# Layer 0's S5 parameter preparation spread among the mixers' turns, LRU first, three column tiles with the first norm

## The chip, the cores and the metric

The kernel runs on one core of one Trainium2 chip. The metric is the device time of one execution in microseconds (us); the kernel before takes 1784.58 us, the median of three runs (1783.12 to 1785.43). Engines: PE is TensorE, DVE VectorE, ACT ScalarE, POOL GpSimd, SP the engine that issues the transfers (DMA).

## What is computed

Two layers of a hybrid backbone over 640 tokens (128 of a context pass, 512 of a denoising step) of 1024 channels, in fp32. Cut to what matters:

```python
mod = silu(cond) @ mod_w + mod_b                    # six vectors of 1024: shift, scale, gate, twice
h = rmsnorm(x, norm1_w) * (1.0 + sc1) + sh1
proj = h @ w_in                                     # 20 column tiles of 128
ya, st_a = ssd_mixer(pa, ...)                       # Mamba-2 SSD, chunks of 128 tokens
yb, st_b = retention_mixer(pb, ...)
yc, st_c = s5_mixer(pc, ...)                        # complex diagonal scan
yd, st_d = lru_mixer(pd, ...)                       # RG-LRU, diagonal scan
y = concatenate([ya, yb, yc, yd]) @ w_out
x = x + g1 * y
h = rmsnorm(x, norm2_w) * (1.0 + sc2) + sh2
x = x + g2 * conv_ffn(h, w_up, conv_w, conv_b, w_down)
```

S5 needs parameters that depend on no token: `abar = exp(lam * step)`, its powers, `bbar = coef * b`, and `c` times powers. The kernel computes them on the chip.

## The kernel before, in words

Activations lie with channels on the partitions, in 8 tiles of 128 channels (k = 0 to 7), each as a high and a low part (`hhi`, `hlo`); weights are split the same way by `wsplit`: SP loads a `raw` page of 128x512, ACT casts it to `hi`, DVE or POOL (by turns) subtracts to `lo`. `mm3` multiplies three of the four pairs. A column tile (`col_tile`) is 128 output columns for all 640 tokens in two halves of 320, each half in a PSUM bank: 8 k x 3 products x 2 halves = 48 matmuls of 128x320, and two raw pages. There are 3 banks for column tiles ("mm"), 1 "a", 2 "b", 1 "c", 1 "mod".

Layer 0 starts with nothing in place. `mod_first(q)` computes the shift and scale for two of the eight k at a time (q = 0 to 3), with matmuls into `mod` and then DVE steps (`modtt`, `modtl`, eight copies of 32x4 into `mod0`). The norm then makes, per k, `nt` on DVE, `hhi` on ACT and `hlo` on DVE or POOL. `first_tiles` (L232) builds the first two column tiles (S5's) quarter by quarter as the norm's channels arrive.

After that each mixer is a generator; `ORDER` lists their turns (L45 of the kernel before), one `yield` to the next per turn, and after each turn `filler` steps the computation of layer 0's other four modulation vectors (`mod_units`, matmuls `mod<-mraw,s`). In layer 0 the S5 mixer goes first, and the whole of `s5_prep(0)` (L577) is emitted behind its first step. `s5_prep` makes powers and tables (`pw`, `tab`, `tbr`), then for each of four q the products `pmr` and `pt` of 128x512 on DVE with `pmi` and `pt` on POOL, transposes on PE (`c`), and copies on ACT (`wbs`, `kt`, `kk`). `s5_mixer` (L773) copies the two column tiles out of PSUM on ACT (`s5cp`, `s5cs`), transposes them (`b`, `s5u`), and runs scans per q (`s5a`, `s5r`) with the prepared matrices (`wb`, `wc`, `tb`). SSD's chunks run as `sE`, `S` and `scb` steps on DVE with PE.

The program's order on each engine is not the emitted one: a scheduler orders instructions by a model of their times, within the dependencies, and pages and banks of one tag are handed out in the emitted order (`fresh`, `last`). An engine runs its queue in that order. All operations pass through one recording helper (L92 before, L90 after), so every row shows that line and the tiles' names tell which step it is.

Of the kernel before, what the change touches and what calls it, by code (L numbers as in the profile page):

```python
# [9 lines left out]
F32 = mybir.dt.float32  # L10
# [7 lines left out]
P = 128  # L18
# [7 lines left out]
HO = (1, 0)  # L26
# [12 lines left out]
TSR = 1  # L39
LB = 1  # L40
FPS = 2
ST = 'AAC'
MR = 'C'

ORDER = ("s5 gb lru lru gb ssd ssd z lru ssd z ret ret ssd ret ssd ret ret ret ret",  # L45
         "s5 ssd gb lru ssd lru gb z lru ssd z ret ssd ret ret ssd ret ret ret ret")
RAWS = 5
SPLITS = 5
# [27 lines left out]
def hybrid_kernel(ctx: ExitStack, tc: tile.TileContext, I, O, dbg=None):  # L76
# [155 lines left out]
    def first_tiles(units, act, steps=None):  # L232


        ws = [wsplit(u, 1024, le=G) for u in units]
        out = [[None, None] for _ in ws]
        for ks in steps or ():
            for h in HO:
                for i, (w, o) in enumerate(zip(ws, out)):
                    if o[h] is None:  # L240
                        o[h] = bank("a" if i and h == HO[1] else "mm")
                    col_tile(w, act, halves=(h,), ks=ks, out=o[h])
        if steps:
            return out
        for h in HO:
            for w, o in zip(ws, out):
                o[h], = col_tile(w, act, halves=(h,))
        return out


    s4 = cst.tile([P, 8, 32], F32, name="s4")
# [7 lines left out]
    def mod_first(q):  # L259

        ps = bank("mod")
        for k in range(8):
            if k % 2 == 0:
                raws = [page(MR, name="mraw")[:, :512] for _ in range(2)]
                for c in range(2):
                    SP.dma_start(raws[c], I["mod0"][q, c, k // 2])
            for c in range(2):
                j = 2 * (k % 2) + c
                T.matmul(ps[32 * j:32 * j + 32, 0:256], s4[:, k, :], raws[c][:, 256 * (k % 2):256 * (k % 2) + 256],
                         start=k < 2, stop=k > 5, tile_position=(0, 32 * j))  # L270
        tt = smp.tile([P, 16, 32], F32, tag="modtt", name="modtt")[:, 0:8]
        V.transpose(tt, ps[:, 0:256].rearrange("p (b r) -> p b r", r=32))
        tl = smp.tile([64, 16, 2], F32, tag="modtl", name="modtl")[:, 0:8]
        V.tensor_copy(tl, tt[64:128, :, 0:2])
        V.tensor_tensor(tl, tl, tt[0:64, :, 0:2], op=ALU.add)
        ks = slice(2 * q, 2 * q + 2)
        for c in range(2):
            src = tl[32 * c:32 * c + 32].rearrange("p (q b) d -> p q b d", b=4)
            for b in range(4):
                V.tensor_copy(mod0[32 * b:32 * b + 32, c, ks, :], src[:, :, b, :])  # L280
        V.tensor_tensor(mod0[:, :, ks], mod0[:, :, ks],
                        pr(0, "mod_b", 0, 16).rearrange("p (c k) -> p c k", c=2)[:, :, ks].unsqueeze(3).to_broadcast(
                            [P, 2, 2, 2]), op=ALU.add)
        mod_scale(0, 0, ks)

    def mod_units(l, c, pages):


        ps = bank("mod")
        after = mybir.DependencyInfo(mybir.DependencyClass.Sync, mybir.DependencyReason.DATA)  # L290
        for k in range(8):
            raws = [page(pages, name="mraw")[:, :512] for _ in range(2)]
            dmas = [SP.dma_start(raws[i], I["mod_w"][l, c, k, :, 512 * i:512 * i + 512]) for i in range(2)]
            for j in range(4):
                mm = T.matmul(ps[32 * j:32 * j + 32, 0:256], s4[:, k, :], raws[j // 2][:, 256 * (j % 2):256 * (j % 2) + 256],
                              start=k == 0, stop=k == 7, tile_position=(0, 32 * j))
                if j < 2:
                    tc.add_manual_dep(mm.ins, dmas[1].ins.name, after, reason="four at a time")
            if k < 7:
                yield  # L300
        tt = smp.tile([P, 16, 32], F32, tag="modtt", name="modtt")[:, :8]
        V.transpose(tt, ps[:, 0:256].rearrange("p (b r) -> p b r", r=32))
        dst = modT[l][c]
        for j in range(4):
            src = tt[32 * j:32 * j + 32, :, 0:2].rearrange("p (q b) c -> p q b c", b=4)
            for b in range(4):
                V.tensor_copy(dst[32 * b:32 * b + 32, 2 * j:2 * j + 2, :], src[:, :, b, :])
        V.tensor_tensor(dst, dst, pr(l, "mod_b", c * 8, 8).unsqueeze(2).to_broadcast([P, 8, 2]), op=ALU.add)
        yield

# [266 lines left out]
    def s5_prep(l):  # L577

        wb, wc, tb, zz = s5d[l]
        p1, p2, p3 = "CCC" if l else ST  # L580

        def keep(name, shape):
            return smp.tile([P] + shape, F32, tag=f"k_{name}", name=name)
# [186 lines left out]
            SP.dma_start(zz[:, :, j, :], kk[16 * j:16 * j + 16, :, 16:32])  # L770


    def s5_mixer(l, hh, y, steps):  # L773
        u = []
        yield
        tiles = first_tiles([I["w_in"][l, 4 + i] for i in range(2)], hh, steps)
        for i in range(2):

            ucp, ucs = paged("B", [2, 4, 32], "s5cp"), paged("B", [2, 2, 4, 32], "s5cs")
            G.memset(ucp, 0.0)  # L780
            with tc.high_priority(EVP):
                for h, t, c0, o, n in ((0, ucp, 0, 0, 128), (0, ucs[:, 0], 0, 128, 192), (1, ucs[:, 0], 24, 0, 64),
                                       (1, ucs[:, 1], 0, 64, 256)):
                    A.copy(t[:, :, :, c0:c0 + n // 8],
                           tiles[i][h][:, o:o + n].rearrange("p (c b j) -> p j b c", b=4, j=2)[:, ::-1, ::-1, :])
            uq = paged("B", [8, TB], "s5u")
            ps = bank("b")
            for j in range(2):
# [134 lines left out]
    def lru_mixer(l, hh, y):  # L923
# [14 lines left out]
        hs = []  # L938
        for i in range(2):
            yield  # L940
            pss = col_tile(wsplit(I["w_in"][l, i], 1024), hh)
            raw = page("A", name="lraw")
            evac_padded(pss, raw)
            xr = page("A", name="lxc")
# [53 lines left out]
    def gates(l, hh, units, out, func):  # L998

        for i in range(2):  # L1000
            yield
            pss = col_tile(wsplit(I["w_in"][l, units[i]], 1024), hh)
            for h in range(2):
                o, w = HALF[h]
                if func is None:
# [334 lines left out]
    def layer(l, norm):  # L1340
# [3 lines left out]
        for ks in steps or (range(8),):  # L1344
            if l == 0 and ks[0]:
                mod_first(ks[0] // 2)
            for h in HO:
                norm.apply(l, 0, h, hh, ks)
        ys = {n: [page(tag, name="y" + n) for _ in range(2)] for n, tag in (("lru", "Ya"), ("ssd", "Yb"), ("s5", "Yc"))}
        ys["ret"] = []  # L1350
        gens = {"s5": s5_mixer(l, hh, ys["s5"], steps), "lru": lru_mixer(l, hh, ys["lru"]), "ssd": ssd_mixer(l, hh, ys["ssd"]),
                "ret": ret_mixer(l, hh, ys["ret"]), "gb": gates(l, hh, (2, 3), ys["lru"], AF.Gelu_apprx_tanh),
                "z": gates(l, hh, (9, 11), ys["ssd"], None if TSZ else AF.Silu)}
        for n in gens:
            if n != "ret":
                step(n + str(l), gens[n])
            if l == 0 and n == "s5":
                step("s50", gens[n])
                sec[0] = "prep"
                for _ in s5_prep(0):  # L1360
                    pass
        order = ORDER[l].split()
        for i, n in enumerate(order):
            if n == "ret" and "ret" not in order[:i]:
# [2 lines left out]
                ys["ret"] += [page("Yd", name="yret") for _ in range(2)]  # L1367
                step(n + str(l), gens[n])
            step(n + str(l), gens[n])
            if i == 0 and l == 0:  # L1370
                load_x(0)
            if l == 0 and i >= 1:
                filler(FPS)
# [348 lines left out]
```

## Time and profile before

| | |
|---|---|
| median of three runs | 1784.58 us (1783.12 to 1785.43) |
| the profiled execution | 1781.99 us, span of its instructions 1780.0 us |
| PE busy | 1662.9 us (93%), 11288 matmuls |
| DVE, ACT, POOL busy | 1117.3 (63%), 683.6 (38%), 610.6 us (34%) |
| mean granted clock of PE | 0.974 of full speed |
| transfers | 206.5 MB, mean 116 GB/s |

A busy share over the whole span mixes stages: the FFN, on PE alone, takes most of it. The rows further down are times from the span's start. In a timeline row a bracket tells how long the engine was idle before the instruction and which one ended that; `x8` are eight instructions merged into one row. [...]

### The profile page before, as it was taken

How to read it: one execution, taken by the hardware profiler on the slowest of the kernel's cores; microseconds unless marked ns; L12 is line 12 of the kernel's file. 1: busy time of each engine (PE TensorE's matmuls, PEld its weight loads, DVE VectorE, ACT ScalarE, POOL GpSimd, SP SyncE). 2: the span in 40 equal slices, each digit the busy share in tenths (PEclk: the TensorE clock that was granted, in tenths of full speed). 3: DMA queues.
4: the chain of work that ended last, by engine and by line, in shares of the span. 5: the costliest groups of instructions: out<-in, count | busy, mean ns of one | idle time of the engine just before them, and what ended most of it. 6: DMA issues, size and time to landing. Idle time of an engine off the chain costs nothing. (4 is left out here: it accounts for less than half of the span.)

```text
span 1780.0 us, 30854 instructions
## 1 busy us (share of the span) xinstructions
PE 1662.9 (93%) x11288; PEld 1525.9 (86%) x11288; DVE 1117.3 (63%) x2605; ACT 683.6 (38%) x1448; POOL 610.6 (34%) x838
## 2 busy tenths in 40 slices
PE   4598998999999999999999999999989999999997
PEld 1386787888998988989998889887889999999996
DVE  9977976977543875584447688687764333333345
ACT  4534424444431352232234464454453233233234
POOL 4665343423311263261123344433331121121222
PEclk8798999999999999999999999999999999999998
DMA  8355565321424354444443334422122222222321
GB/s 308 112 182 157 165 202 171 96 81 46 139 81 154 123 173 148 155 152 134 151 138 107 95 121 132 130 85 70 35 63 63 75 84 64 91 72 62 93 73 59
DMA packets 143434, 206.50 MB, mean 116 GB/s; under 512 B 22852, under 2 KB 64692, under 8 KB 143284
## 3 DMA queue, kind: packets, MB, share of 16 engines
q1 hardware_dynamic: 143284, 204.54, 36.7%
q8 instruction: 89, 1.46, 0.3%
q14 instruction: 61, 0.50, 0.1%
HBM read 184.42 MB, written 20.07 MB: 115 GB/s over the span
## 5 line engine op out<-in xcount | busy, mean ns | idle before, releaser
L92 PE MATMUL mm<-hhi,hi 128*128 128x320 f32 x1976 | 625.1, 317 | 34.6 <-ACT hhi L92 28.2
L92 PE MATMUL mm<-hlo,hi 128*128 128x320 f32 x1976 | 627.0, 318 | 7.5 <-DVE hlo L92 4.8
L92 PE MATMUL mm<-hhi,lo 128*128 128x320 f32 x1976 | 619.3, 314 | 1.1 <-DVE lo L92 1.1
L92 ACT CAST hi<-raw 128x512 fp32r<-128x512 f32 (+1 forms) x384 | 227.5, 593 | 606.6 <-PE mm L92 404.1
L92 POOL TENSOR_TENSOR lo<-raw,hi 128x512 fp32r<-128x512 f32 (+1 forms) x200 | 260.4, 1303 | 580.8 <-ACT hi L92 563.2
L92 PEld LDWEIGHTS mm<-hhi,hi 128*128 128x128 f32 x1976 | 376.1, 191 | 58.4 <-ACT hhi L92 33.5
L92 PEld LDWEIGHTS mm<-hlo,hi 128*128 128x128 f32 x1976 | 376.6, 191 | 19.0 <-DVE hlo L92 6.9
L92 PEld LDWEIGHTS mm<-hhi,lo 128*128 128x128 f32 x1976 | 376.7, 191 | 5.4 <-issue 2.4
L92 DVE TENSOR_TENSOR lo<-raw,hi 128x512 fp32r<-128x512 f32 (+1 forms) x184 | 133.7, 727 | 180.9 <-ACT hi L92 165.3
L92 DVE SCALAR_TENSOR_TENSOR x<-mm,mod,x 128x320 f32<-128x320 f32 (+2 forms) x288 | 116.9, 434 | 203.0 <-PE mm L92 201.9
L92 PE MATMUL mm<-fah,hi 128*128 128x320 f32 x640 | 196.8, 313 | 1.0 <-DVE fa L92 0.7
L92 PE MATMUL mm<-fal,hi 128*128 128x320 f32 x640 | 197.4, 309 | 0.0
L92 PE MATMUL mm<-fah,lo 128*128 128x320 f32 x640 | 196.7, 309 | 0.0
L92 PEld LDWEIGHTS mm<-fah,hi 128*128 128x128 f32 x640 | 119.3, 188 | 11.7 <-issue 7.6
L92 PEld LDWEIGHTS mm<-fah,lo 128*128 128x128 f32 x640 | 120.2, 188 | 0.4 <-issue 0.4
L92 PEld LDWEIGHTS mm<-fal,hi 128*128 128x128 f32 x640 | 120.3, 188 | 0.2 <-issue 0.2
L92 DVE TENSOR_TENSOR fa<-fc,mm 128x128 f32<-128x128 f32 x132 | 45.1, 373 | 106.7 <-PE mm L92 103.4
L92 PE MATMUL mod<-mraw,s 128*32 128x256 f32 x768 | 74.4, 414 | 17.5 <-DMA mraw<-in_mod 13.6
L92 DVE SCALAR_TENSOR_TENSOR fc<-fraw,par,fc 128x643 f32<-128x643 f32 x88 | 84.6, 963 | 2.8
L92 POOL MEMSET fraw<- 128x2 f32 x132 | 8.8, 102 | 173.1 <-DVE fc L92 167.3
L92 PE MATMUL mm<-ylo,hi 128*128 128x320 f32 x192 | 61.5, 321 | 1.8 <-DVE ylo L92 1.8
L92 PE MATMUL mm<-yhi,hi 128*128 128x320 f32 x192 | 61.9, 326 | 0.6 <-DVE x L92 0.4
(363 smaller groups left out, 2619.4 us busy)
## 6 DMA issues: line engine op xcount, KB each, us to landing
raw<-in_up SPq DMA_DIRECT2D x176, 256.0 KB
mraw<-in_mod_w SPq DMA_DIRECT2D x160, 256.0 KB
raw<-in_w_in SPq DMA_DIRECT2D x80, 256.0 KB
raw<-in_dn SPq DMA_DIRECT2D x96, 192.0 KB
mraw<-in_mod SPq DMA_DIRECT2D x32, 256.0 KB
raw<-in_w_o SPq DMA_DIRECT2D x32, 256.0 KB
tb<-tb SPq DMA_DIRECT2D x16, 326.0 KB
x<-in_x SPq DMA_DIRECT2D x16, 320.0 KB
```

Source lines behind the costliest of these rows:

```text
L92: r = f(*a, **k)
```

## The change

`ORDER[0]` puts LRU first and S5 behind LRU's third turn; `p` is one step of `s5_prep(0)`, of which there are ten turns. The preparation's large pages come from "B" (12 pages, where S5's `s5cp`, `s5cs` and `s5u` also lie) instead of "A" and "C". The first norm is followed by three column tiles instead of two, LRU's two and the first of its gate, kept in `early` until their turn fetches them (`unit_tile`); the third tile's weight parts lie in pages "A", and the `lo` parts go to DVE and POOL by turns. Layer 1 still starts with S5's two. `mod_first` copies the PSUM rows out on ACT, transposes them on PE into bank "c" and adds them on DVE in two steps. Layer 0's remaining modulation vectors are placed by ACT copies instead of DVE copies. `load_x(0)` follows the second S5 turn instead of the first turn.

```diff
--- before.py
+++ after.py
@@ -39,10 +39,8 @@
 TSR = 1
 LB = 1
 FPS = 2
-ST = 'AAC'
-MR = 'C'
-
-ORDER = ("s5 gb lru lru gb ssd ssd z lru ssd z ret ret ssd ret ssd ret ret ret ret",
+
+ORDER = ("lru p gb p lru p gb p ssd p ssd p z p lru p p p s5 s5 ssd z ret ret ssd ret ssd ret ret ret ret",
          "s5 ssd gb lru ssd lru gb z lru ssd z ret ssd ret ret ssd ret ret ret ret")
 RAWS = 5
 SPLITS = 5
@@ -232,13 +230,14 @@
     def first_tiles(units, act, steps=None):
 
 
-        ws = [wsplit(u, 1024, le=G) for u in units]
+        ws = [wsplit(u, 1024, le=None if steps else G, tag="A" if i > 1 else None) for i, u in enumerate(units)]
         out = [[None, None] for _ in ws]
+        banks = (("mm", "mm"), ("b", "b"), ("a", "mm"))
         for ks in steps or ():
             for h in HO:
                 for i, (w, o) in enumerate(zip(ws, out)):
                     if o[h] is None:
-                        o[h] = bank("a" if i and h == HO[1] else "mm")
+                        o[h] = bank(banks[i][h])
                     col_tile(w, act, halves=(h,), ks=ks, out=o[h])
         if steps:
             return out
@@ -247,6 +246,12 @@
                 o[h], = col_tile(w, act, halves=(h,))
         return out
 
+    early = {}
+
+    def unit_tile(l, u, hh):
+
+        return early.pop((l, u), None) or col_tile(wsplit(I["w_in"][l, u], 1024), hh)
+
 
     s4 = cst.tile([P, 8, 32], F32, name="s4")
     G.memset(s4, 0.0)
@@ -261,26 +266,25 @@
         ps = bank("mod")
         for k in range(8):
             if k % 2 == 0:
-                raws = [page(MR, name="mraw")[:, :512] for _ in range(2)]
+                raws = [page("AC"[q % 2], name="mraw")[:, :512] for _ in range(2)]
                 for c in range(2):
                     SP.dma_start(raws[c], I["mod0"][q, c, k // 2])
             for c in range(2):
                 j = 2 * (k % 2) + c
                 T.matmul(ps[32 * j:32 * j + 32, 0:256], s4[:, k, :], raws[c][:, 256 * (k % 2):256 * (k % 2) + 256],
                          start=k < 2, stop=k > 5, tile_position=(0, 32 * j))
-        tt = smp.tile([P, 16, 32], F32, tag="modtt", name="modtt")[:, 0:8]
-        V.transpose(tt, ps[:, 0:256].rearrange("p (b r) -> p b r", r=32))
-        tl = smp.tile([64, 16, 2], F32, tag="modtl", name="modtl")[:, 0:8]
-        V.tensor_copy(tl, tt[64:128, :, 0:2])
-        V.tensor_tensor(tl, tl, tt[0:64, :, 0:2], op=ALU.add)
+
+        rows = smp.tile([P, 512], F32, tag="modtt", name="modtt")[:, 0:256]
+        A.copy(rows, ps[:, 0:256])
+        ps = bank("c")
+        for i in range(2):
+            T.transpose(ps[:, 128 * i:128 * i + 128], rows[:, 128 * i:128 * i + 128], idn)
         ks = slice(2 * q, 2 * q + 2)
-        for c in range(2):
-            src = tl[32 * c:32 * c + 32].rearrange("p (q b) d -> p q b d", b=4)
-            for b in range(4):
-                V.tensor_copy(mod0[32 * b:32 * b + 32, c, ks, :], src[:, :, b, :])
-        V.tensor_tensor(mod0[:, :, ks], mod0[:, :, ks],
+        src = ps[:, 0:256].rearrange("p (k j r) -> p j k r", k=2, j=4)[:, :, :, 0:2]
+        V.tensor_tensor(mod0[:, :, ks], src[:, 0:2],
                         pr(0, "mod_b", 0, 16).rearrange("p (c k) -> p c k", c=2)[:, :, ks].unsqueeze(3).to_broadcast(
                             [P, 2, 2, 2]), op=ALU.add)
+        V.tensor_tensor(mod0[:, :, ks], mod0[:, :, ks], src[:, 2:4], op=ALU.add)
         mod_scale(0, 0, ks)
 
     def mod_units(l, c, pages):
@@ -304,7 +308,8 @@
         for j in range(4):
             src = tt[32 * j:32 * j + 32, :, 0:2].rearrange("p (q b) c -> p q b c", b=4)
             for b in range(4):
-                V.tensor_copy(dst[32 * b:32 * b + 32, 2 * j:2 * j + 2, :], src[:, :, b, :])
+                cp = A.copy if pages == "Yd" else V.tensor_copy
+                cp(dst[32 * b:32 * b + 32, 2 * j:2 * j + 2, :], src[:, :, b, :])
         V.tensor_tensor(dst, dst, pr(l, "mod_b", c * 8, 8).unsqueeze(2).to_broadcast([P, 8, 2]), op=ALU.add)
         yield
 
@@ -577,7 +582,7 @@
     def s5_prep(l):
 
         wb, wc, tb, zz = s5d[l]
-        p1, p2, p3 = "CCC" if l else ST
+        p1 = p2 = p3 = "C" if l else "B"
 
         def keep(name, shape):
             return smp.tile([P] + shape, F32, tag=f"k_{name}", name=name)
@@ -770,11 +775,11 @@
             SP.dma_start(zz[:, :, j, :], kk[16 * j:16 * j + 16, :, 16:32])
 
 
-    def s5_mixer(l, hh, y, steps):
+    def s5_mixer(l, hh, y):
         u = []
         yield
-        tiles = first_tiles([I["w_in"][l, 4 + i] for i in range(2)], hh, steps)
         for i in range(2):
+            tl = unit_tile(l, 4 + i, hh)
 
             ucp, ucs = paged("B", [2, 4, 32], "s5cp"), paged("B", [2, 2, 4, 32], "s5cs")
             G.memset(ucp, 0.0)
@@ -782,7 +787,7 @@
                 for h, t, c0, o, n in ((0, ucp, 0, 0, 128), (0, ucs[:, 0], 0, 128, 192), (1, ucs[:, 0], 24, 0, 64),
                                        (1, ucs[:, 1], 0, 64, 256)):
                     A.copy(t[:, :, :, c0:c0 + n // 8],
-                           tiles[i][h][:, o:o + n].rearrange("p (c b j) -> p j b c", b=4, j=2)[:, ::-1, ::-1, :])
+                           tl[h][:, o:o + n].rearrange("p (c b j) -> p j b c", b=4, j=2)[:, ::-1, ::-1, :])
             uq = paged("B", [8, TB], "s5u")
             ps = bank("b")
             for j in range(2):
@@ -938,7 +943,7 @@
         hs = []
         for i in range(2):
             yield
-            pss = col_tile(wsplit(I["w_in"][l, i], 1024), hh)
+            pss = unit_tile(l, i, hh)
             raw = page("A", name="lraw")
             evac_padded(pss, raw)
             xr = page("A", name="lxc")
@@ -999,7 +1004,7 @@
 
         for i in range(2):
             yield
-            pss = col_tile(wsplit(I["w_in"][l, units[i]], 1024), hh)
+            pss = unit_tile(l, units[i], hh)
             for h in range(2):
                 o, w = HALF[h]
                 if func is None:
@@ -1346,19 +1351,19 @@
                 mod_first(ks[0] // 2)
             for h in HO:
                 norm.apply(l, 0, h, hh, ks)
+        us = (0, 1, 2) if l == 0 else (4, 5)
+        for u, t in zip(us, first_tiles([I["w_in"][l, u] for u in us], hh, steps)):
+            early[l, u] = t
         ys = {n: [page(tag, name="y" + n) for _ in range(2)] for n, tag in (("lru", "Ya"), ("ssd", "Yb"), ("s5", "Yc"))}
         ys["ret"] = []
-        gens = {"s5": s5_mixer(l, hh, ys["s5"], steps), "lru": lru_mixer(l, hh, ys["lru"]), "ssd": ssd_mixer(l, hh, ys["ssd"]),
+        gens = {"s5": s5_mixer(l, hh, ys["s5"]), "lru": lru_mixer(l, hh, ys["lru"]), "ssd": ssd_mixer(l, hh, ys["ssd"]),
                 "ret": ret_mixer(l, hh, ys["ret"]), "gb": gates(l, hh, (2, 3), ys["lru"], AF.Gelu_apprx_tanh),
                 "z": gates(l, hh, (9, 11), ys["ssd"], None if TSZ else AF.Silu)}
         for n in gens:
             if n != "ret":
                 step(n + str(l), gens[n])
-            if l == 0 and n == "s5":
-                step("s50", gens[n])
-                sec[0] = "prep"
-                for _ in s5_prep(0):
-                    pass
+        if l == 0:
+            gens["p"] = s5_prep(0)
         order = ORDER[l].split()
         for i, n in enumerate(order):
             if n == "ret" and "ret" not in order[:i]:
@@ -1367,7 +1372,7 @@
                 ys["ret"] += [page("Yd", name="yret") for _ in range(2)]
                 step(n + str(l), gens[n])
             step(n + str(l), gens[n])
-            if i == 0 and l == 0:
+            if l == 0 and n == "s5" and "s5" in order[:i]:
                 load_x(0)
             if l == 0 and i >= 1:
                 filler(FPS)
```

How this moves instructions, at three places.

DVE in the first norm, the last quarter (q = 3) of `mod_first`, before (`modtt`, `modtl` are its temporaries, `mod0_87` its result, `am` the scale, `nt` the normed activations, `tab` the preparation's tables):

```order
L92 TENSOR_TENSOR modtl_465<-modtl_465,modtt_463 64x16
L92 TENSOR_TENSOR tabt_946<-tab1_945,e5_859 128x256
L92 COPY s5ph_0_112<-tab1_945 64x8
L92 COPY mod0_87<-modtl_465 32x4 x8
L92 TENSOR_TENSOR tab0_944<-tab0_944,tabt_946 128x8x32
L92 TENSOR_TENSOR mod0_87<-mod0_87,par0_75 128x2x4
L92 SCALAR_TENSOR_TENSOR am0_0_98<-mod0_87,par0_75 128x4
L92 TENSOR_SCALAR am0_0_98<-am0_0_98 128x4
L92 SCALAR_TENSOR_TENSOR nt_479<-x_131,am0_0_98,nrs_136 128x320
L92 SCALAR_TENSOR_TENSOR nt_483<-x_133,am0_0_98,nrs_136 128x320
```

and now:

```order
L90 TENSOR_TENSOR wlo_502<-raw_499,whi_501 128x512
L90 TENSOR_TENSOR mod0_87<-c_444,par0_75 128x2x4
L90 TENSOR_TENSOR tabt_1319<-tab1_1318,e1_1115 128x8x2
L90 TENSOR_TENSOR mod0_87<-mod0_87,c_444 128x2x4
L90 TENSOR_TENSOR tab0_1317<-tab0_1317,tabt_1319 128x8x2
L90 SCALAR_TENSOR_TENSOR am0_0_98<-mod0_87,par0_75 128x4
L90 TENSOR_TENSOR lo_1240<-raw_1237,hi_1239 128x512
L90 TENSOR_TENSOR tab0_1317<-tab0_1317,e2_1120 128x8x4
L90 TENSOR_SCALAR am0_0_98<-am0_0_98 128x4
L90 TENSOR_TENSOR tabt_1319<-tab1_1318,e2_1120 128x8x4
L90 SCALAR_TENSOR_TENSOR nt_451<-x_131,am0_0_98,nrs_136 128x320
L90 SCALAR_TENSOR_TENSOR nt_455<-x_133,am0_0_98,nrs_136 128x320
```

The transpose, the copy, the add and the eight small copies are gone from DVE; two adds that read the transposed PSUM bank `c` stand in their place, with weight splits (`wlo`, `lo`) and table steps between.

PE ahead of S5's second column tile, now (`pmr_2003` and `pmi_2004` are the products of the preparation's last q, `mm_2174` is the second half of S5's second column tile; its first half, `mm_2173`, stands 77 rows earlier, behind both halves of the first tile):

```order
L90 MATMUL mod_1605<-mraw_1614,s4_84 32x256 x2
L90 MATMUL mod_1605<-mraw_1615,s4_84 32x256 x2
L90 MATMUL c_2031<-pmr_2003,cm0_1596 32x128 x4
L90 MATMUL c_2031<-pmi_2004,cm1_1597 32x128 x4
L90 MATMUL c_2042<-ct_72,kt_2040 128x128
L90 MATMUL mod_1605<-mraw_1698,s4_84 32x256 x2
L90 MATMUL mod_1605<-mraw_1699,s4_84 32x256 x2
L90 MATMUL mm_2174<-hhi_237,hi_2163 128x320
L90 MATMUL mm_2174<-hlo_238,hi_2163 128x320
L90 MATMUL mm_2174<-hhi_237,lo_2164 128x320
```

Before, S5's tiles were the first column tiles of the program, ahead of all the preparation's transposes; now the transposes of all four q stand between the first three halves and the fourth.

ACT where S5's tiles are copied out of their banks, before (`mm_533` is the second half of S5's first column tile, `tbr` and `cm0` are preparation):

```order
L92 COPY tbr_1005<-tab1_945 64x4x64
L92 ACTIVATE hhi_258<-nt_495,mod0_87 128x192
L92 COPY s5cs_634<-mm_533 128x8x8
L92 COPY s5cs_634<-mm_533 128x256
L92 ACTIVATE nt_495<-nt_495,mod0_87 128x128
L92 COPY tbr_1005<-tab1_945 64x4x64
L92 COPY cm0_1035<-cq_1022 64x16x16 x2
L92 COPY cm1_1036<-ncq_1033 64x16x16 x2
```

and now (`mm_2092` and `mm_2093` are the first tile's halves; `kk` is the preparation's last result per q):

```order
L90 COPY wbs_2018<-c_2013 128x512
L90 COPY wbs_2027<-c_2022 128x512
L90 COPY kt_2040<-c_2031 128x128
L90 COPY kk_1604<-c_2042 128x128
L90 COPY s5cs_2143<-mm_2093 128x8x8
L90 COPY s5cs_2143<-mm_2093 128x256
L90 COPY s5cp_2142<-mm_2092 128x8x16
L90 COPY s5cs_2143<-mm_2092 128x8x24
L90 CAST hi_2780<-raw_2778 128x512
```

The copies that give S5's banks free stood ahead of the first `kk`; they now stand behind the last of the four.

## Rows read from the trace of the kernel before

**Rows 1.** Stretches: start:end, length, busy PE, PEld, DVE, ACT, POOL, clock, DMA share, GB/s

```profile
0.00:50.00 50.00, 22.83 (x128) 10.78 (x128) 45.77 (x260) 21.83 (x49) 22.20 (x41) 0.86 0.85 300
...
50.00:100.00 50.00, 32.89 (x161) 25.70 (x162) 38.47 (x93) 27.80 (x75) 29.86 (x45) 0.76 0.29 96
...
431.10:1780.00 1348.90, 1301.51 (x8885) 1230.28 (x8883) 765.74 (x1675) 494.87 (x1029) 409.03 (x567) 0.99 0.34 104
```

**Rows 2.** Stretches of layer 0's mixers, columns as above

```profile
100.00:200.00 100.00, 90.10 (x629) 70.73 (x628) 85.41 (x152) 41.11 (x77) 61.40 (x79) 0.95 0.62 186
...
184.50:431.10 246.60, 230.10 (x1586) 200.02 (x1585) 196.44 (x472) 103.02 (x232) 94.15 (x119) 0.99 0.41 128
```

**Rows 3.** Waits of PE, 0 to 300 us: total, times, longest

```profile
PE mm L92 <- ACT hhi L92: 24.9, 6, 10.2
...
PE c L92 <- DVE sE L92: 3.8, 1, 3.8
```

**Rows 4.** Timeline of PE, first column tiles: start, us, instruction

```profile
68.25 0.31 PE L92 MATMUL mm<-hhi,hi 128*128 128x320 f32 x1
68.40 0.31 PE L92 MATMUL a<-hhi,hi 128*128 128x320 f32 x1
78.90 0.90 PE L92 MATMUL mm<-hhi,hi 128*128 128x320 f32 x2 [10.19 <-ACT hhi L92]
...
93.45 0.47 PE L92 MATMUL mm<-hhi,hi 128*128 128x320 f32 x1
93.72 0.47 PE L92 MATMUL mm<-hlo,hi 128*128 128x320 f32 x1
...
113.98 0.31 PE L92 MATMUL mm<-hhi,lo 128*128 128x320 f32 x1
```

**Rows 5.** Stretch of the first norm's activations

```profile
33.50:84.80 51.30, 31.52 (x150) 20.08 (x150) 48.93 (x142) 25.06 (x65) 37.00 (x59) 0.71 0.37 123
```

**Rows 6.** Timeline of DVE, first norm

```profile
27.82 2.68 DVE L92 COPY mod<-modtl 32x4 f32<-32x4 f32 x8
...
33.51 2.02 DVE L92 SCALAR_TENSOR_TENSOR nt<-x,am,nrs 128x320 f32<-128x320 f32 x2
...
73.12 2.98 DVE L92 COPY mod<-modtl 32x4 f32<-32x4 f32 x8
...
84.82 2.55 DVE L92 SCALAR_TENSOR_TENSOR nt<-x,am,nrs 128x128 f32<-128x128 f32 x2
```

**Rows 7.** Groups of DVE, 24 to 88 us: busy, mean ns, idle before

```profile
L92 DVE COPY mod<-modtl 32x4 f32<-32x4 f32 x32 | 8.2, 255 | 0.4
...
L92 DVE COPY modtl<-modtt 64x16 f32<-64x16 f32 x4 | 1.6, 396 | 0.1
...
L92 DVE TENSOR_TENSOR lo<-raw,hi 128x512 fp32r<-128x512 f32 x2 | 1.3, 674 | 0.0
...
L92 DVE STREAM_TRANSPOSE modtt<-mod 128x256 f32<-128x256 f32 x3 | 1.3, 440 | 0.0
...
L92 DVE TENSOR_TENSOR modtl<-modtl,modtt 64x16 f32<-64x16 f32 x4 | 1.1, 283 | 0.0
```

**Rows 8.** Groups of DVE, 85 to 200 us; ACT, 24 to 200 us

```profile
L92 DVE TENSOR_TENSOR pt<-ncq,apcw 128x512 f32<-128x512 f32 x4 | 5.5, 1382 | 0.0
...
L92 DVE TENSOR_TENSOR_SCAN lg<-lg,lT 128x644 f32<-128x644 f32 x2 | 3.0, 1496 | 0.0
...
L92 ACT COPY tbr<-tab 64x68 f32<-64x68 f32 x16 | 4.0, 248 | 1.7 <-DVE tab L92 0.7 <-POOL tab L92 0.6
```

**Rows 9.** Timeline of DVE, the preparation's products

```profile
87.30 0.68 DVE L92 TENSOR_TENSOR pt<-bb,apcw 128x512 f32<-128x512 f32 x1
...
105.35 1.54 DVE L92 TENSOR_TENSOR pmr<-bb,apcw 128x512 f32<-128x512 f32 x1
```

**Rows 10.** Groups of DVE, 200 to 330 us

```profile
L92 DVE TENSOR_TENSOR_SCAN s5r<-tb,s5a 64x328 f32<-64x328 f32 x8 | 6.7, 836 | 1.1 <-POOL s5a L92 0.9
...
L92 DVE SCALAR_TENSOR_TENSOR sE<-scb,cum,sE 128x128 f32<-128x128 f32 x12 | 4.9, 443 | 0.0
```

## The prediction

> **What bounds the kernel now.** I read the page's totals through a table of stretches first: where is TensorE (PE) not busy? From 431.1 us on, PE is busy 1301.5 of 1348.9 us [rows 1], so there is nothing to gain there except by starting it earlier; and since the order of instructions is the same in both programs from the second half of layer 0's output projection on, a lead gained before it is carried to the end one for one. The first 100 us hold two rows of 50 us with 22.8 and 32.9 us of PE work [rows 1]: 44 us idle. From 100 to 431 us the idle share is small: 9.9 us in 100 to 200 and 16.5 us in 184.5 to 431.1 [rows 2]. So the whole case lies before 431 us, most of it before 115.
>
> The waits say what PE lacks there: 24.9 us for `hhi`, the normed activations' high part, in 6 waits, the longest 10.2 [rows 3]. The timeline shows that one: PE stops behind 68.40 and goes on at 78.90 [rows 4]. ACT makes `hhi` from `nt`, which VectorE (DVE) makes, and DVE is busy 48.9 of the 51.3 us from the first `nt` to the last [rows 5]. **DVE sets the pace of the first norm**, and one piece stands out: at 73.12 eight copies of 32x4 take 2.98 us, and nt can't start before them [rows 6].
>
> **The first norm's stage.** For each of four quarters `mod_first` now runs a DVE transpose, a copy, an add and eight small copies: 1.3 + 0.4 (the fourth transpose, at the mean of the three), 1.6, 1.1 and 8.2 us, 12.3 in all [rows 7]. The change gives this to an ACT copy and two PE transposes; DVE keeps the bias add and gets a second one of the same size, which I price at the 0.28 us of the old add [rows 7], 1.1 us together. The saving is 11.2 us, 2.8 per quarter. The first quarter's copies stand at 27.82, before the first `nt` at 33.51 [rows 6]; I take 4 us off (2.8 and the steps that queue behind them), so the first `nt` at 29.5. The other three quarters save 8.4. The split of the third tile adds DVE work: five `lo` of 0.67 us instead of two [rows 7], +2.0. The preparation's first product `pmr`, 1.4 us at the price of its kind [rows 8], and four steps of half its width, taken as the same again, move behind the norm: -2.8. So 9.2 of 48.9 us go, and at the same pace (51.3 us for 48.9) the last `nt` comes at 29.5 + 41.6 = **71 us, against 84.82** [rows 6].
>
> PE must follow. The six raw pages of three tiles instead of four stand ahead of the first tile matmul's ACT cast, so it starts a few us later; that costs nothing as long as the last `nt` decides, and PE has 35 us for the 144 matmuls, which take 21 us at a spacing of 0.15 us (68.25 to 68.40) and 39 at the 0.27 of 93.45 to 93.72 [rows 4]. Three tiles are then finished at about 76. The fourth is one more set of 48 matmuls, 7 us at the one spacing and 13 at the other: 85. Before, the fourth tile ends at 114 [rows 4]. **Lead: 29 us** (22 to 31, by the two spacings).
>
> **The preparation's block.** This is what the lead runs into. `ORDER` puts three turns of `p` ahead of the two of `s5`, but the scheduler starts S5's two column tiles long before: their halves hold all three `mm` banks, and the next tile (`mm` 2174) waits until ACT copies one out. ACT does so behind the last of `kk`, the preparation's product, and in pages "B" that the preparation holds too (the order's pieces on PE and ACT). Before, these tiles had the banks first and were copied out ahead of the first `kk`. So PE now waits for DVE's chain from the last `nt` to the last `pmr`. I count that chain in the change's order: 24 products `pmr` and `pt` at 1.38 [rows 8] are 33; LRU's two tiles (conv, gates, scans, sums; the scan alone 1.50 [rows 8]) 27; SSD's first conv and step sizes 12; five `lo` 4; the tables' tail and `bb` 8; the rest 2: 86 us. A product takes 0.68 us at 87.30, where POOL has none, and 1.54 at 105.35, where POOL runs its own [rows 9]; the change leaves the pairs side by side, so I keep 1.38.
>
> If DVE never waited, the last `pmr` would end at 71 + 86 = 157. It is busy 85.4 us of 100 here [rows 2], which makes 171.5, and the way through transpose, `kt`, `kk` and the bank's copy (four short ACT copies like the 0.25 of [rows 8] among them) adds some 4: **hold ends at 175 us**. Behind it lie 217 us of PE work by row durations, and in the trace of before that much is left at 184.5. The lead is down to **9.5 us** (24 if DVE never waits; 2 if it is busy only 0.8).
>
> **What is left of it.** From 184.5 to 431.1 us before has 230.1 of 246.6 us PE busy and 196.4 DVE busy [rows 2]; the change has the same matmuls there and about 192 us of DVE work, since layer 0's 48 remaining copies of 32x4 go to ACT, which is busy 103 of 246.6 [rows 2]. I put this part at zero, with a loss of 20 us as one bound (below) and PE's 16.5 idle us [rows 2] as the other; zero, because the work on both engines is the same within 3%. `load_x(0)`, now behind the second S5 turn, and the "AC" pages for `mraw` cost nothing: the transfers' load is down to 0.62 in 100 to 200 us [rows 2], and `x` is next read by the output projection's sums.
>
> On the copies sent to ACT: a row gives DVE 255 ns each [rows 7], so 48 are worth 12 us of DVE; ACT's nearest row, a copy of 64x68, takes 248 ns [rows 8], 12 us on an engine that is busy 42%. [...]
>
> **Sum.** 29 gained, 19.5 given back at the preparation, 0 behind it: 9.5 us off the profiled execution's 1781.99, 1772.5. That execution stands 2.6 us below the median of the runs, which makes **1775 us** against 1784.58.
>
> **The rivals.**
> (a) *Slower: S5 late beside SSD.* S5's eight scan groups move behind the preparation and fall on the start of SSD's chunks. In the change's order there is a stretch in which DVE has 33 us of row durations (six scans of 0.84, some thirty `sE` steps like those of 0.44 [rows 10], and the rest of both mixers' steps) and PE 13 between two `b` tiles that DVE must read. If PE has nothing else to run, 20 us are lost and the time is 1775 + 20 = 1795. For it: PE's queue is in order, and before the longest wait of PE in this part is of this kind, 3.8 us for `sE` [rows 3]. Against it: DVE's total there is no larger than before. It decides once DVE's work between those two tiles exceeds PE's by 14 us. [...]
> (b) *No hold.* DVE keeps ahead, because LRU and SSD give it work without waits: hold ends at 161, lead 24, 1761. Against it: DVE is 15% idle here before, with much the same steps [rows 2].
> (c) *No difference.* The order's later turns simply use up the 9.5 us, because DVE (86 and 192 us, against PE's 60 from the fourth tile to the hold and 217 behind it) is as much a bound as PE: 1782 to 1788.
>
> **How the numbers follow.** About 3.6 us (0.2%) is what a measurement of this kernel can tell from no change. Forecast 0.42, rival (a) 0.30, (b) 0.14, (c) 0.14. Faster: 0.42 + 0.14 = 0.56; same 0.14; slower 0.30. The likeliest case's own range is 1767 to 1781; with (b) in full and (a) in full it is 1758 to 1797.
>
> **What would show it.** Right: last `nt` near 71 us, no 10 us wait for `hhi`, the fourth tile done by 85 to 90; then a wait of `mm` on ACT's `s5cs` or `s5cp` until about 175; the FFN's first matmul near 422. Wrong: the `mm` wait missing (then b), DVE waiting much longer than 15 us between 71 and 171 (lead gone), a wait of several us of `c` or `b` on `sE` or `s5r` in 200 to 300 (a), or the last `nt` still behind 80, in which case the first step failed.

## The result and the profile after

The changed kernel takes 1808.5 us, the median of four runs (1805.86 to 1810.25), against 1783.85 of the kernel before beside it (1782.94 to 1785.43): ratio 1.0136 [1.0118, 1.0154], 1.4% slower, where 0.5% faster was forecast. (The brackets hold a 95% interval.) The profiled span is 1806.8 us at a mean granted clock of 0.959 (before 1780.0 at 0.974).

Stretches of the kernel after, columns as in [rows 1]:

```profile
0.00:50.00 50.00, 24.17 (x153) 10.78 (x153) 43.97 (x254) 25.30 (x59) 21.92 (x42) 0.86 0.79 285
50.00:100.00 50.00, 43.03 (x266) 37.53 (x265) 36.06 (x66) 29.49 (x72) 31.29 (x49) 0.90 0.52 164
...
150.00:200.00 50.00, 24.64 (x183) 14.10 (x182) 29.85 (x35) 17.27 (x46) 26.13 (x31) 0.66 0.56 167
131.00:194.00 63.00, 32.12 (x211) 13.95 (x204) 40.98 (x46) 24.62 (x68) 36.02 (x39) 0.64 0.54 165
260.00:302.00 42.00, 30.80 (x169) 27.66 (x168) 38.25 (x103) 14.11 (x38) 20.64 (x38) 0.67 0.45 126
```

The second row is the promised gain: 43.0 us of PE work against 32.9 [rows 1]. The fourth row pays it back: from 131 to 194 us PE is busy 32 of 63 us, and DVE, which was to set the pace there, only 41. The same stretches before:

```profile
131.00:194.00 63.00, 57.04 (x379) 42.87 (x382) 50.88 (x103) 30.64 (x56) 32.28 (x48) 0.92 0.59 169
260.00:302.00 42.00, 35.41 (x235) 27.85 (x235) 25.57 (x93) 12.40 (x35) 11.60 (x14) 0.92 0.53 181
```

DVE's timeline after, first norm (before: [rows 6], first `nt` 33.51, last 84.82) and the preparation's first product:

```profile
28.97 1.16 DVE L90 SCALAR_TENSOR_TENSOR nt<-x,am,nrs 128x320 f32<-128x320 f32 x2
...
71.75 1.25 DVE L90 SCALAR_TENSOR_TENSOR nt<-x,am,nrs 128x128 f32<-128x128 f32 x2
...
80.09 0.69 DVE L90 TENSOR_TENSOR pmr<-bb,apcw 128x512 f32<-128x512 f32 x1
```

The first product stands at 80, but its transposes wait 50 us. PE's timeline after:

```profile
130.11 0.66 PE L90 MATMUL c<-ct,pmr 128*128 128x128 f32 x4 [0.17 <-ACT dtc L90]
...
168.12 1.08 PE L90 MATMUL c<-ct,pmr 128*128 128x128 f32 x4 [6.17 <-DVE pmr L90]
...
192.31 1.06 PE L90 MATMUL mod<-mraw,s 128*32 128x256 f32 x8 [2.40 <-DMA mraw<-in_mod_w]
193.29 0.64 PE L90 MATMUL mm<-hhi,hi 128*128 128x320 f32 x1
```

ACT's timeline after, with what released that wait, and the `kk` copies that end the four rounds:

```profile
129.80 0.25 ACT L90 COPY dtc<-c 40x128 f32<-40x128 f32 x1
...
139.47 0.27 ACT L90 COPY kk<-c 128x128 f32<-128x128 f32 x1 [0.87 <-PE c L90]
...
159.72 0.27 ACT L90 COPY kk<-c 128x128 f32<-128x128 f32 x1 [0.57 <-PE c L90]
...
178.38 0.27 ACT L90 COPY kk<-c 128x128 f32<-128x128 f32 x1 [4.97 <-PE c L90]
...
189.94 0.27 ACT L90 COPY kk<-c 128x128 f32<-128x128 f32 x1 [0.42 <-PE c L90]
190.11 0.49 ACT L90 COPY s5cs<-mm 128x64 f32<-128x64 f32 x2
```

There is one bank "c", handed out in emitted order. `ORDER` emits two SSD turns ahead of the rounds (a round is the work on one of the four q), so the round's transposes stand behind SSD's step sizes, whose last copy out of `c` is `dtc` at 129.80. The same copies before, on ACT:

```profile
105.71 0.27 ACT L92 COPY kk<-c 128x128 f32<-128x128 f32 x1 [2.98 <-PE c L92]
124.39 0.27 ACT L92 COPY kk<-c 128x128 f32<-128x128 f32 x1 [1.96 <-PE c L92]
141.00 0.26 ACT L92 COPY kk<-c 128x128 f32<-128x128 f32 x1
152.57 0.26 ACT L92 COPY kk<-c 128x128 f32<-128x128 f32 x1
```

That is 15.6 us per round before and 16.8 after. The rounds are nearly as fast; the first is 34 us late.

The waits of PE after, 0 to 480 us (total, times, longest) and, last, 100 to 200 us:

```profile
PE mod L90 <- DMA mraw<-in_mod_w: 20.4, 11, 4.5
...
PE c L90 <- DVE pmr L90: 6.2, 1, 6.2
...
PE a L90 <- DVE sE L90: 4.1, 1, 4.1
PE b L90 <- DMA wc<-wc: 4.0, 1, 4.0
```

```profile
PE mod L90 <- DMA mraw<-in_mod_w: 18.0, 8, 4.5
```

Of the 24.9 us for `hhi` [rows 3] 0.3 are left. In their place PE waits for the modulation weights inside the hold, since those matmuls stand in its queue there, between the rounds' transposes.

**Where the time went.** The table gives the start of the same amount of PE work left before the FFN's down product (an estimate: each matmul at one duration for its shape, at the full clock), against the kernel before; minus is ahead. Next to a long wait another choice of these durations moves an entry by several us; the row of 70 hardly depends on them. Columns are kernels of the experiments below.

| PE us left | after | e5 | g2 | f2 | h1 |
|---|---|---|---|---|---|
| 350 | -22.3 | -19.9 | -21.2 | -21.1 | -11.0 |
| 330 | -33.6 | +3.1 | -25.4 | -9.0 | -4.7 |
| 310 | +10.1 | +5.1 | -12.8 | -4.8 | -4.8 |
| 250 | +7.0 | +4.8 | -15.9 | -4.8 | -8.9 |
| 230 | +18.1 | +12.4 | -7.4 | -5.7 | -11.6 |
| 180 | +27.4 | +19.7 | +0.3 | -5.1 | -8.6 |
| 70 | +26.7 | +19.5 | +0.8 | -3.9 | -6.5 |

Two losses: 43.7 us in the hold (330 to 310 left), the stretch in which PE can't go on with column tiles, and 16.6 behind it (from 10.1 to 26.7 behind), which falls between 250 and 180 left.

### The profile page after: what moved, and what is told of

Same layout as the page of the kernel before. It is cut to its first block, busy times and chain, and to the rows that moved or that the text cites. A ratio compares the mean times of both kernels' runs of the same rounds, so it can differ in the third digit from the quotient of the medians.

```text
span 1806.8 us, 30836 instructions
## 1 busy us (share of the span) xinstructions
PE 1671.8 (93%) x11296; PEld 1537.5 (85%) x11296; DVE 1089.2 (60%) x2519; ACT 697.5 (39%) x1502; POOL 602.1 (33%) x836
## 3 DMA queue, kind: packets, MB, share of 16 engines
q8 instruction: 90, 1.47, 0.3%
## 4 chain that ended last, share of the span: by engine, by line
PE 70%; DVE 17%; DMA 4%; ACT 3%; issue 3%; POOL 2%; SPq 0%; DVEq 0%; POOLq 0%; ACTq 0%
PE mm L90 59%; PE b L90 6%; PE mod L90 3%; PE c L90 2%; DVE nt L90 2%; PE a L90 1%; DMA mraw<-in_mod_w 1%; DVE sE L90 1%; DVE s L90 1%; DVE x L90 1%; DVE pmr L90 1%; DVE lo L90 1%; DVE s5r L90 1%; DVE nacc L90 1%; DVE fc L90 1%
## 5 line engine op out<-in xcount | busy, mean ns | idle before, releaser
L90 PE MATMUL mm<-hhi,hi 128*128 128x320 f32 x1952 | 616.9, 317 | 16.9 <-ACT hhi L90 3.3
L90 PE MATMUL mm<-hlo,hi 128*128 128x320 f32 x1952 | 617.4, 317 | 6.3 <-DVE hlo L90 3.6
L90 PE MATMUL mm<-hhi,lo 128*128 128x320 f32 x1952 | 610.3, 313 | 0.0
L90 POOL TENSOR_TENSOR lo<-raw,hi 128x512 fp32r<-128x512 f32 (+1 forms) x197 | 254.9, 1294 | 618.8 <-ACT hi L90 580.4
L90 PEld LDWEIGHTS mm<-hhi,hi 128*128 128x128 f32 x1952 | 371.6, 191 | 37.1 <-issue 18.0
L90 PEld LDWEIGHTS mm<-hlo,hi 128*128 128x128 f32 x1952 | 371.5, 190 | 14.3 <-POOL hlo L90 5.2
L90 PEld LDWEIGHTS mm<-hhi,lo 128*128 128x128 f32 x1952 | 371.4, 190 | 5.2 <-issue 2.8
L90 PEld LDWEIGHTS mod<-mraw,s 128*32 128x32 f32 x768 | 19.5, 116 | 60.0 <-issue 26.4
```

Of the source, the lines that this page charges most:

```text
L90: r = f(*a, **k)
```

## The experiments

Ratios are against the kernel before on the same chip. The start of the last `kk` of each kernel (153 in the kernel before, 190 after) tells when the preparation ended.

**1. Is it the order of the turns, or the fillers?** e5 lets the rounds and S5 precede SSD; e4 takes S5's first turn, with both its tiles, early, which frees their banks; h2 puts three of the four rounds ahead of SSD; e2 steps no modulation filler behind a `p`.

```diff
 change: "lru p gb p lru p gb p ssd p ssd p z p lru p p p s5 s5 ssd z ret ..."
+e5: "lru p gb p lru p gb p lru p p p p p p s5 s5 ssd ssd z ssd z ret ..."
+e4: "lru p gb s5 p lru p gb p ssd p ssd p z p lru p p p s5 ssd z ret ..."
+h2: "lru p gb p lru p gb p p p p p ssd ssd z lru p p s5 s5 ssd z ret ..."
-            if l == 0 and i >= 1:
+e2:         if l == 0 and i >= 1 and n != "p":
```

> The change with all ten turns of the preparation and both S5 turns ahead of SSD's turns, so S5's scans no longer meet SSD's chunks. Theory 'S5 beside SSD' (19 us lost behind 260 us, 11 of them from 260 to 302): these come back, 1787 to 1795 us, the hold staying as it is, since S5's tiles still wait for the preparation. Rival (these losses only follow from the time at which PE runs out of column tiles): no gain, 1803 to 1812.

> The change with S5's first turn (its two tiles, copied out of their banks) moved up behind the first gate turn, ahead of all but one turn of the preparation. Theory 'banks': no hold, the 44 us lost between 131 and 194 come back by 25 to 44 us, 1765 to 1783 us, if the later losses stay. Rival 'filler' or 'pages': PE still waits behind the transposes, within 8 us of the change, 1800 to 1808.

> The change with the first three rounds of products emitted ahead of SSD's first two turns and of LRU's third; S5 still behind those SSD turns. Theory 'bank c and queues' (the rounds share PSUM's one c bank with SSD's step sizes, handed out in the emitted order, and wait for SSD's chain): the first kk comes at 105 instead of 139.5, the third by 150, the last by 175, PE's hold ends 15 us earlier or more, and the time is 1785 to 1800. Rival (rounds are slow because LRU's scans stand between them on DVE): the first kk moves but the last stays behind 185, 1803 to 1812.

> The change, with no filler step on the ten turns of the preparation, so fewer modulation matmuls stand in PE's queue between its transposes. Theory 'banks' (PE starves from 131 to 193 us because S5's tiles hold all mm banks until the preparation is done): the stretch shortens by 5 us or so, 1800 to 1806 us. Rival 'filler' (PE's waits for mraw, 20.4 us in 11, make the stretch): those waits go and the time falls by about 20, to 1788.

e5: 1.0107 [1.0077, 1.0137]. On ACT:

```profile
102.74 0.27 ACT L90 COPY kk<-c 128x128 f32<-128x128 f32 x1
...
158.37 0.27 ACT L90 COPY kk<-c 128x128 f32<-128x128 f32 x1 [0.56 <-PE c L90]
```

Without SSD ahead, the first round ends 37 us earlier and the last 31. About a third of that reaches the end (span 1796.2 against 1806.8), and the time, 1799.4 us, lies between both forecasts; PE is still held, only earlier (busy 31.8 of 60 us from 100 to 160). No run gave the rounds a bank of their own, so that it is bank "c" in particular rests on the kernel's rule of emitted order and on PE's row at 130.11; that the place behind SSD delays the rounds is shown.

e4: 1.0392 [1.0364, 1.0420], outside both forecasts. PE isn't held until about 185 us and is up to 40 us ahead, but the preparation moves back (first `kk` 194.4, last 248.8) and the hold comes later (PE busy 36.3 of 75 us from 185 to 260). Freeing S5's banks this way gains nothing; since the edit moved the preparation too, it doesn't tell what a free bank alone is worth.

h2: 1.0174 [1.0149, 1.0200]. Three rounds end by 147.8; the one left behind SSD waits for its copy again, and the end is where it was, which is the rival's forecast (last `kk` behind 185). ACT's timeline of h2:

```profile
147.77 0.27 ACT L90 COPY kk<-c 128x128 f32<-128x128 f32 x1
...
176.61 0.26 ACT L90 COPY dtc<-c 40x128 f32<-40x128 f32 x1 [0.49 <-PE c L90]
...
188.89 0.27 ACT L90 COPY kk<-c 128x128 f32<-128x128 f32 x1 [3.00 <-PE c L90]
```

e2: 1.0170 [1.0145, 1.0194]. PE waits 9.9 us for `mraw` in 100 to 200 us instead of 18.0, last `kk` 189.6, and the time is no better: those waits fill a time that is lost anyway.

**2. Is it the "B" pages?** f1 is the kernel before with its preparation's pages from "B" alone; e1 is the changed kernel with S5 first, two tiles, the whole preparation behind S5's first turn, as before, and no filler behind a `p`; f2 is e1 with the old pages; f3 and g2 take the third set of pages from "C", in the change's order and in e5's.

```diff
-ST = 'AAC'
+f1: ST = 'BBB'
-ORDER = ("lru p gb p lru p gb p ssd ...
+e1, f2: ORDER = ("s5 p p p p p p p p p p s5 gb lru lru gb ssd ssd z lru ...
-        us = (0, 1, 2) if l == 0 else (4, 5)
+e1, f2: us = (4, 5)
+e1, f2: banks = (("mm", "mm"), ("a", "mm"))
+e1, f2: if l == 0 and i >= 1 and n != "p":
-        p1 = p2 = p3 = "C" if l else "B"
+f2:     p1, p2, p3 = "CCC" if l else "AAC"
+f3, g2: p1, p2, p3 = "CCC" if l else "BBC"
```

> The kernel before with one edit: the preparation's pages all from B. Theory 'pages' (five rotating pages make each of the four rounds of products wait for the round trip of the one before): the last kk comes 15 to 35 us later than at 152.6, and the time goes up by about as much, 1795 to 1815 us. Rival 'order' (the pages are enough where the preparation stands alone): within 5 us of the kernel before.

> The turns stand as in the kernel before (S5's two tiles with the norm and copied out first, the preparation as one block behind them, filler on the other turns alone); mod_first, the ACT copies, the B pages of the preparation and its splits stay as changed. Theory 'order' (the whole loss comes from where S5 and its preparation stand): 1770 to 1785 us, no wait of the column tiles for S5's banks, and a first norm some 10 us shorter than before. Rival 'pages' (the preparation's five rotating B pages make its chain long wherever it stands): 1795 or more, with DVE and POOL waiting for the transfers of wbs as in the change.

> The first experiment (turns as in the kernel before) with the preparation's pages back to A, A and C, so of the change only mod_first, the ACT copies, the splits by turns and the place of load_x are left. Theory 'end of the preparation decides': the last kk comes at 140 to 155 us and the time is 1768 to 1783. Rival (one of the other edits costs): 1795 or more.

> The change with the preparation's products in C pages instead of B. Theory 'pages': rounds of 14 to 16 us instead of 20, the hold of PE ends 10 to 20 us earlier than 193, 1785 to 1798 us. Rival 'order' (the rounds are slow because PE's and ACT's queues hold other mixers' work between their steps): 1802 to 1810.

> The change with the preparation and S5 ahead of SSD (as in the fourth experiment) and the preparation's products in C pages. Theory 'end of the preparation decides': SSD does not use the C pages yet, the last kk comes by 150 instead of 158.4 and the time is 1785 to 1793. Rival (pages no longer matter in this order): within 4 us of the fourth experiment, 1.0107 times the kernel before.

f1: 1.0317 [1.0296, 1.0337]. The pages alone, in the old program, cost more than the whole change, and more than was forecast. They too are handed out in emitted order, so the preparation's first table waits until S5's tiles have been transposed: `pw` starts at 79.14 on DVE (19.95 before), the first product at 117.4, the last `kk` comes at 220.2 (before: 152.6). Half of these 68 us is that late start, which was not foreseen (first `kk` 138.0 against 105.7); the other half is the rounds, as theory 'pages' said: 27.4 us each against 15.6. On DVE:

```profile
79.14 0.20 DVE L92 TENSOR_TENSOR pw<-u,mag 128x32 f32<-128x32 f32 x1
...
117.36 0.67 DVE L92 TENSOR_TENSOR pmr<-bb,apcw 128x512 f32<-128x512 f32 x1
```

e1, 1.0274 [1.0254, 1.0295], against f2, 0.9975 [0.9965, 0.9986]: 3% again, with last `kk` 212.6 and 145.1, and 26.7 against 15.8 us per round. In the change's own order f3 gives 1.0173 [1.0148, 1.0198], no better: the first round stays behind SSD whatever its pages (`kk` 138.9). In e5's order the pages count: g2, 0.9989 [0.9980, 0.9998], against e5's 1.0107, with the last `kk` at 152.9 (1779.5 us, better than the 1785 to 1793 forecast). So **order and pages cover each other**: either one alone mended brings 0.3% (e5, with overlapping intervals) or nothing (f3), both together 1.5%.

**3. Is it the products' work, or SSD beside S5?** g4 leaves two thirds of the products' work out (one step of three in each). g3 puts four turns of `p` first, h3 moves SSD's later turns behind retention's first ones.

```diff
-            cmul([wide(bb[:, i]) for i in range(2)], [pwr(v) for v in ap], pm, tt)
+g4:         V.tensor_tensor(pm[0], wide(bb[:, 0]), pwr(ap[0]), op=M_)
+g4:         G.tensor_tensor(pm[1], wide(bb[:, 1]), pwr(ap[0]), op=M_)
-            V.tensor_tensor(tt[0], wide(ncq), pwr(cw[1]), op=M_)
...
+g3: "p p p p lru p p gb p lru p p p s5 s5 gb lru ssd ssd z ssd z ret ...", pages "BBC"
+h3: "... lru p p p s5 s5 z ret ret ssd ret ssd ret ssd ret ret ret"
```

> The change with only the first of the three steps of each of the preparation's products on DVE and POOL, so two thirds of that work is left out (some 22 us of DVE and of POOL) and with it the other products' share of bbar and c. Theory 'queues' (the rounds are slow because their steps wait for one another through PE, ACT, the transfers and pages): the last kk still comes behind 175, 1795 to 1806 us. Rival 'work' (DVE and POOL are the bound, as forecast): the last kk comes by 168, 1780 to 1790.

> Three column tiles with the norm as in the change, but four turns of the preparation ahead of LRU, the other six between LRU's and the gate's turns, then S5, then SSD; products in C pages. Theory 'end of the preparation decides': last kk by 145, 1770 to 1785 us, the best of the orders with LRU first. Rival (LRU first costs by itself, because S5's scans then meet SSD's chunks): 1790 or more although the last kk is early.

> The change with SSD's chunk turns moved behind the first retention turns, so that S5's scans meet retention's column tiles instead of SSD's chunks. Theory 'S5 beside SSD' (DVE has 33 us of work there against PE's 13): the 11 us lost between 260 and 302 us come back at least in part, 1795 to 1803 us. Rival 'mixers' work' (DVE's work behind the hold is the bound in any order): it is lost later instead, 1805 to 1815.

g4: 1.0104 [1.0089, 1.0120], `kk` from 137.6 to 166.0. The start stays, the rounds shrink to 9.5 us each; 24 us earlier gives 11 us of span. By the last `kk` (by 168) that is the forecast of 'work', by the time (1800.5 us) that of 'queues': the products' work sets the length of a round, but two thirds of it left out gives back less than half of the loss. PE is 12.5 us ahead at 310 left and still ends 21.8 behind. g3: 1.0071 [1.0054, 1.0087], last `kk` 158.8 instead of the 145 forecast, so it tests neither theory. h3: 1.0190 [1.0172, 1.0209]; the second loss stays (at 230 left it is 32 us behind before). Moving SSD away doesn't bring it back, as the rival 'mixers' work' had it.

**4. What are the parts worth that were to gain?** On the kernel before: f4 has only the new `mod_first`, g1 only the ACT copies in `mod_units`, h1 both.

```diff
 f4, h1: mod_first as in the change, pages from MR as before
-                V.tensor_copy(dst[32 * b:32 * b + 32, 2 * j:2 * j + 2, :], src[:, :, b, :])
+g1, h1:         cp = A.copy if pages == "Yd" else V.tensor_copy
+g1, h1:         cp(dst[32 * b:32 * b + 32, 2 * j:2 * j + 2, :], src[:, :, b, :])
```

> The kernel before with mod_first of the change and nothing else. The last nt moves from 84.8 to about 72 us by its own price. Theory 'end of the preparation decides': the preparation follows the norm on DVE, its last kk moves by half of that or more, 1770 to 1779 us against a median of before near 1780. Rival (the norm's end is not on the path): within 3 us of the kernel before.

> The kernel before with layer 0's 48 small copies of the remaining modulation vectors on ACT and nothing else. By the rows of DVE (0.16 to 0.26 us each) it frees some 10 us of DVE; theory 'end of the preparation decides': most of them stand behind the preparation, so within 4 us of the kernel before. Rival 'ACT's queue' (sixteen copies in a row, 3.2 us, stand in ACT's queue ahead of the preparation's copies and of the activations): 3 to 8 us slower.

> The kernel before with mod_first of the change and the ACT copies, nothing else. If the two parts add, 0.995 x 0.998 = 0.993 of the kernel before, some 1769 us; if the ACT copies only filled time that the shorter norm opens, 0.995, some 1773.

f4: 0.9951 [0.9934, 0.9968]; g1: 0.9980 [0.9968, 0.9991]; h1: 0.9941 [0.9924, 0.9958], 1770.47 us, the lowest median here and faster than both kernels of the comparison. The intervals of f4 and h1 overlap, so what the copies add to f4 isn't settled. In h1 the last `nt` starts at 78, the last `kk` at 149.7. Its first stretches:

```profile
0.00:50.00 50.00, 25.98 (x132) 12.65 (x132) 43.75 (x241) 23.10 (x52) 25.87 (x44) 0.90 0.87 304
50.00:100.00 50.00, 40.61 (x255) 31.24 (x253) 36.09 (x82) 30.48 (x83) 33.48 (x49) 0.86 0.42 133
```

Its 40.6 us of PE work in 50 to 100 us are nearly the change's 43.0, with two tiles and S5 first. The change's own advantage there, 11 us more of lead at 350 left than h1, is worth nothing at the end in any order tried.

All kernels by the last `kk` and the span:

| kernel | f2 | f4 | h1 | g1 | before | g2 | e5 | g3 | g4 | h2 | e2 | h3 | after | f3 | e1 | f1 | e4 |
|---|---|---|---|---|---|---|---|---|---|---|---|---|---|---|---|---|---|
| last `kk` | 145 | 146 | 150 | 152 | 153 | 153 | 158 | 159 | 166 | 189 | 190 | 190 | 190 | 199 | 213 | 220 | 249 |
| span | 1775 | 1771 | 1774 | 1777 | 1780 | 1781 | 1796 | 1789 | 1796 | 1816 | 1805 | 1818 | 1807 | 1809 | 1827 | 1839 | 1847 |

The span goes with the end of the preparation, hardly with PE's lead at 100 us. That is an association, and a loose one: h2 and h3 end the preparation when the change does and are 9 and 11 us longer. Pairs that differ in one thing alone bear it out in direction: pages, before to f1 (68 us later, 59 lost), e1 to f2 (68 earlier, 53 gained) and e5 to g2 (5 earlier, 16 gained); work, the change to g4 (24 earlier, 11 gained).

## Why the prediction was wrong

The forecast was 1775 us (1758 to 1797) with 0.56 on faster; it came out 24.7 us slower, outside the range, on the side of rival (a).

- **First norm: right.** First `nt` 28.97 (predicted 29.5), last 71.75 (71). PE's fourth tile ends at 89.6 (85), a lead of 24.6 us, inside the 22 to 31 given. The bias adds cost 0.16 us each, not 0.28. f4 shows that the mechanism holds by itself: its last `nt` comes at 75.92, 8.9 us earlier than before. Two slips in the sum don't matter: the DVE steps listed add up to 12.6 us, not 12.3, and the slower spacing gives a lead of 25, not 22.
- **Preparation's block: the place was right, the working wrong.** The step that failed is "If DVE never waited, the last `pmr` would end at 71 + 86 = 157. It is busy 85.4 us of 100 here [rows 2], which makes 171.5". It treats the block as DVE work to be got through. From 131 to 194 us DVE is busy 41.0 of 63 us; its 21 products there take 22.4 us, 1.07 each, not 1.38. What sets the pace is a row of waits: the first round for bank "c" behind SSD's `dtc` (129.8), then in turn `wb` transfers, POOL and modulation weights. DVE's waits in 131 to 194 us:

```profile
DVE pmr L90 <- DMA wb<-wbs: 5.2, 1, 5.2
DVE lg L90 <- ACT lg L90: 3.3, 2, 3.0
DVE modtt L90 <- PE mod L90: 2.7, 1, 2.7
DVE pmr L90 <- POOL pmi L90: 2.5, 1, 2.5
```

  The hold ended at 193.3, not 175. Nor did the sign come that was named for it, a wait of `mm` on `s5cs` or `s5cp`: what stands ahead of the next tile in PE's queue are the rounds' transposes and the modulation's matmuls, and ACT's copies at 190.11 are done before PE gets there. The order showed the chain (the SSD turns ahead of the rounds, one bank); I read it for `mm` and not for `c`. An estimate from these rows, one round's 9 us from the release at 130 to its `kk` and three more at the 15.6 of before, gives 186; it came at 190.
- **"I put this part at zero": wrong by 16.6 us.** Rival (a) priced it at 20. In 260 to 302 us DVE is busy 38.3 of 42 us, with S5's scans beside SSD (25.6 before at the same times), while PE has 30.8 us of work. It waits 4.0 us there for `wc` (0.2 before), S5's matrices, which the preparation stores and a transfer brings back; at 344.73 it waits 4.1 for `sE`. The mean granted clock is 0.67 of full speed (0.92 before), and matmuls of one kind take longer than before in the same times: `c<-scb,S` 462 ns against 300, `c<-sE,xk` 444 against 298. The hold, with PE busy 32.1 of 63 us, has a clock of 0.64 (0.92 before); in 302 to 332 us, with PE busy 30.0 of 30, it is 1.00. What lowers it was not shown. The forecast priced no change of the clock. From 250 to 180 left, by the estimate of the table, PE is busy 10 us longer for the same amount of work (after, then before; columns as in [rows 1]):

```profile
256.70:359.30 102.60, 86.18 (x528) 75.83 (x527) 77.60 (x212) 40.22 (x104) 43.95 (x61) 0.82 0.40 121
247.60:332.10 84.50, 76.26 (x542) 64.79 (x543) 63.69 (x164) 31.70 (x84) 35.34 (x42) 0.96 0.48 155
```

  In e5, g2 and h3 it is busy 82 to 87 us there, at clocks of 0.82 to 0.90; in f2, with S5 first, 77.6 at 0.96. So about half of this loss goes with the lower clock (0.82 against 0.96), which a count of the engines' work doesn't show. e5 and g2 lose 14 us too behind 310 left; of f2 and h1, with S5 first, one loses 1 and one gains 2. So this loss goes with LRU-first orders, hold or no hold. Its size is near rival (a)'s, but (a)'s reason isn't borne out: with SSD's later turns moved away (h3) it stayed. Which part of these orders starts it stays open, since g4 didn't remove it either.
- **Copies on ACT: the step held.** 48 take 9.2 us on ACT (191 ns each); on DVE they took 10.2 us before (213 ns each; 12 were predicted). g1's gain of 0.2% is on the side that the rows gave.
- **"A lead gained is carried to the end one for one": right where the prediction placed it**, from the output projection on: the FFN's first matmul comes 26.0 us later than before (457.1; 422 was predicted) and the span is 26.8 us longer. Ahead of that it isn't: 33.6 us of lead came to nothing.

Sum: predicted 9.5 ahead, measured 26.7 behind, 36.2 apart: 19.6 at the block (lead +9.5 predicted, -10.1 found), 16.6 behind it.

## What to carry to other kernels

When a piece of work is spread among others, look at every tag with one or few slots that it shares with them: banks and pages handed out in emitted order chain unrelated work, and a slot that one neighbour holds stops the piece however free its engine is. Follow the longest dependent chain of a stage from its start under those slots before adding up an engine's busy time. An early lead of one engine is only worth what the stage's last chain lets through; the two small edits, one that shortened the chain of the first norm (f4) and one that took copies off DVE (g1), gained 0.5% and 0.2%, the rearrangement around them lost.

## What the runs showed of the hardware

Two sizes were not expected. A DVE add of 128x8 out of a PSUM bank takes 0.16 us, less than the 0.28 of the old add of 64x16 from SBUF [rows 7]. And the products' mean fell to 1.07 us although the pairs stayed, where DVE and POOL were out of step: 0.69 us at 152.95, where POOL is idle, against 1.53 at 162.58, where POOL runs its `pmi`. Elsewhere too: 0.69 us at 80.09, where POOL has a MEMSET, against 1.47 at 170.87 in e4 and 1.43 at 218.61 in f1, where POOL runs a product or sum of its own. The factor of two is that of these rows; what it comes from was not shown.
